# Two-layer streaming step: the heads' stage as four lanes, and written order on all engines between the layers

## The chip, the cores and the metric

The kernel runs on 1 core of one Trainium2 chip. The metric is the device time of one execution in microseconds, as the median of several runs. Engines are called as in the profile: PE (TensorE, matmuls), DVE (VectorE), ACT (ScalarE), POOL (GpSimd) and SP (SyncE, which here only issues DMAs). POOL issues DMAs too.

## The reference

A step of a two-layer encoder over 640 tokens (a prompt of 512 and 8 running streams of 16), with D = 2048, in fp32. Layer 0 is stick-breaking attention with 16 heads. Layer 1 is gated linear attention (GLA) with 4 heads, keys of 256 and values of 512 per head. What the change touches is the end of layer 0 and layer 1:

```
h = rmsnorm(x, norm_g[i]) * (1 + scale) + shift
q, k, v, r, a_lr = split(h @ w_in)                       # layer 1
g = log_sigmoid(a_lr @ w_a2 + b_a) / 16                  # decay, b = cumsum(g) in a chunk
a = tril((q * exp(b)) @ (k * exp(-b)).T)
o = a @ v + (q * exp(b)) @ S
S = exp(b_last) * S + (k * exp(b_last - b)).T @ v
o = o * rsqrt(mean(o * o)) * g_out
y = (o * silu(r)) @ w_out
x = x + gate * y
```

The outputs are y, the new keys and values of layer 0, the final GLA state of the prompt, and the 8 updated states of the streams (8 x 4 heads x 256 x 512 floats, read and written).

## The kernel before

**Arithmetic.** An fp32 product is three matmuls of halves: high x high, high x low, low x high. `halves(hi, lo, x)` (L133) makes them: ACT casts x to hi (L134), DVE subtracts hi from x (L135). Weights come as raw pieces of 128 x 1024 (`wr`, two slots) and are split into `wh`, `wl` by the same pair.

**Stages.** (1) The input is loaded, turned and scaled, and the modulation vectors are computed (to about 165 us). (2) `by_sevens` multiplies by the input weights of layer 0 with seven products in place of eight: it works on sums and differences of quarters of h and of the weights (L514), to about 960 us. `Quarters` holds the parts of h, and `add_up` makes the sums (`sx`, L410) and their halves (`sums`). (3) Attention runs between the first three shares of layer 0's output projection (to about 1450 us). A `share` (L588 on, products L602) is one quarter of the inner dimension of the output projection: four column blocks, in each of them five token tiles, two weight pieces. (4) The last share of layer 0 adds gate and residual (`add`, three DVE operations, L1126 to L1128), squares on ACT (`junk`, L1131), and `turn` brings the tiles into columns (L1112, L1114). `norm` makes the reciprocal root mean square of a tile: a reduce and a mean square on DVE, a power on POOL (L229, `nrm_r`), a widening on DVE (L236), a turn on PE (L238). `scaled` (L244 to L250) applies norm, scale and shift: DVE and ACT for the prompt's part, POOL for the sample's part. (5) `six` (L448) makes the values of GLA head 0 in eight pieces j, `low` (L1189) makes a_lr, `plain` (L560) makes the queries of head 0. (6) `by_sevens` of layer 1 (1660 to 2089 us) makes the other projections by a list of `jobs`: keys, queries, then for each head gates and values. Values are turned into rows by PE (`as_rows`, L583) and stored. (7) The heads' stage (2089 to 2587 us): the rest of the queries and keys by `plain` as filler, then shares 0 to 2 of the layer's output projection as filler, and between their matmuls the four GLA heads. (8) The last share with the final norm (L1652, to the end).

**The order of the work.** PE follows the written order in the whole kernel. A planner (`Side`) counts an estimated PE clock `pe["now"]` while the program is written: lanes (generators) yield `step(wait, tp, z, tiled)`, that is, when they may go on and how many banks of accumulators they need, and `drive` places them between the matmuls of the filler. `side.until` lets the lanes run without a filler. DVE, ACT, POOL and SP take an order that a scheduler derives from the written program; this order is fixed in the built program. `load` and `store` issue DMAs on SP (L70, L73), `move` issues them on POOL (L77).

**The heads before.** A generator `heads` takes the heads one after the other: `decayed` (decays of one head), then `prompt_lane` (four blocks of 128 tokens: L1323, L1311) and `sample_lane` side by side. `sample_lane` handles 16 groups of states in all: four `s0` tiles of 128 x 512 are read (six buffers, loads on SP), multiplied with the queries (L1522) and updated (L1528, DVE L1530), then stored by POOL. `normed` normalizes an output (`on`, with a power on POOL, `on_r`), and `leave` turns it (L1344) and multiplies it with the gates `sr` (L1346). When a head is done, its four rows of blocks (`og`) go to memory or, for the last head and half of heads 1 and 2, straight into halves (`ogh`, `ogl`). `fetch_og` reads the stored ones back before a share.

## Time and profile before

| what | value |
|---|---|
| median of 3 runs | 2663.24 us (2654.84 to 2666.6) |
| the profiled execution | 2674.77 us |
| its span | 2673.1 us |
| its mean granted clock of PE | 0.966 |
| PE busy | 2491.7 us (93%) |
| DVE busy | 1607.2 us (60%) |
| ACT busy | 1005.3 us (38%) |
| POOL busy | 218.0 us (8%) |
| DMA | 498.58 MB, mean 187 GB/s |

The profile is of one execution, which took 11.5 us more than the median. A row of the timeline gives start, length, engine, line, operation, output and inputs, count, and in brackets the idle time of the engine before it with what ended it. A row of waits gives the sum of such idle times, how often, and the longest. Line numbers are those of the kernel before.

### The profile page before, as it was taken

The numbers are of one execution on the slowest core, as the hardware profiler recorded it, in microseconds if no ns is written. First come the engines' busy times: TensorE is split into PE (matmuls) and PEld (weight loads), VectorE is DVE, ScalarE is ACT, GpSimd is POOL, SyncE is SP. The second block draws the span as 40 slices with busy tenths as digits, with TensorE's granted clock in tenths as the row PEclk, the third lists the DMA queues.
The fourth block names the chain that finished last, engine by engine and source line by source line (L and its number), as shares of the span: only waits on it lengthen the run. The fifth ranks groups of instructions, "written<-read, shape, count | busy, mean of one in ns | idle before, by whom it ended". The sixth has DMA issues, their size and how long they took to land.

```text
span 2673.1 us, 43709 instructions
## 1 busy us (share of the span) xinstructions
PE 2491.7 (93%) x17393; PEld 2167.2 (81%) x17393; DVE 1607.2 (60%) x2398; ACT 1005.3 (38%) x1756; POOL 218.0 (8%) x440
## 2 busy tenths in 40 slices
PE   6889999999999989999999789999999799799877
PEld 4569999989999988777777658999999778576655
DVE  4555555565556646666775683666667454455557
ACT  4332222222223335565443452333333334352333
POOL 1200000000000000000000340000000121212113
PEclk8899999999999999999999989999999899899998
DMA  9966666766664376667665533333443666657354
GB/s 324 308 211 212 224 202 214 231 201 217 218 211 139 105 236 214 215 216 244 198 208 165 168 92 107 104 113 106 130 135 104 212 210 216 196 171 225 124 172 162
DMA packets 495549, 498.58 MB, mean 187 GB/s; under 512 B 25130, under 2 KB 415666, under 8 KB 494706
## 3 DMA queue, kind: packets, MB, share of 16 engines
q1 hardware_dynamic: 486066, 465.90, 55.5%
q0 software_dynamic: 9280, 29.89, 3.2%
q8 instruction: 137, 2.24, 0.3%
q14 instruction: 66, 0.54, 0.1%
HBM read 408.54 MB, written 87.16 MB: 185 GB/s over the span
## 4 chain that ended last, share of the span: by engine, by line
PE 74%; DVE 7%; DMA 7%; issue 5%; POOL 3%; ACT 2%; SPq 1%; POOLq 0%; ACTq 0%; DVEq 0%
PE ps_mm L514 41%; PE ps_mm L602 11%; PE ps_mm L560 3%; PE ps_mm L448 3%; PE ps_tp L956 2%; DMA s<-in_state_gla_dram 1%; SPq L70 1%; PE ps_z L900 1%; PE ps_tp L924 1%; PE ps_z L177 1%; PE ps_z L217 1%; DMA ar<-in_w_ada_dram 1%; PE ps_z L969 1%; PE ps_tp L1001 1%; PE ps_tp L1311 1%
## 5 line engine op out<-in xcount | busy, mean ns | idle before, releaser
L514 PE MATMUL ps_mm<-sums,wh 128*128 128x320 f32 x2880 | 643.4, 311 | 2.7 <-ACT wh L134 2.7
L514 PEld LDWEIGHTS ps_mm<-sums,wh 128*128 128x128 f32 x2880 | 480.6, 188 | 14.8 <-issue 9.5
L514 PE MATMUL ps_mm<-h,wh 128*128 128x320 f32 x2160 | 482.7, 311 | 0.6 <-ACT wh L134 0.3
L514 PE MATMUL ps_mm<-sums,wl 128*128 128x320 f32 x1440 | 445.8, 310 | 1.4 <-DVE wl L135 1.4
L135 DVE TENSOR_TENSOR wl<-wr,wh 128x1024 fp32r<-128x1024 f32 x195 | 239.6, 1230 | 251.1 <-ACT wh L134 247.3
L514 PEld LDWEIGHTS ps_mm<-h,wh 128*128 128x128 f32 x2160 | 359.2, 188 | 16.1 <-issue 10.4
L134 ACT CAST wh<-wb 128x1024 fp32r<-128x1024 f32 x180 | 188.9, 1049 | 466.5 <-PE ps_mm L514 401.3
L134 ACT CAST wh<-wr 128x1024 fp32r<-128x1024 f32 x195 | 204.3, 1049 | 385.6 <-PE ps_mm L514 202.4
L514 PE MATMUL ps_mm<-h,wl 128*128 128x320 f32 x1080 | 333.8, 309 | 0.7 <-DVE wl L135 0.7
L514 PEld LDWEIGHTS ps_mm<-sums,wl 128*128 128x128 f32 x1440 | 271.0, 188 | 1.9 <-DVE wl L135 1.9
L135 DVE TENSOR_TENSOR wl<-wb,wh 128x1024 fp32r<-128x1024 f32 x180 | 220.0, 1222 | 63.3 <-ACT wh L134 62.8
L602 PE MATMUL ps_mm<-wh,ogh 128*128 128x512 f32 x530 | 233.4, 440 | 26.4 <-ACT ogh L134 19.0
L560 PE MATMUL ps_mm<-h,wh 128*128 128x320 f32 x896 | 209.8, 322 | 11.4 <-DVE kr L135 8.8
L602 PE MATMUL ps_mm<-wh,ogl 128*128 128x512 f32 x530 | 212.7, 401 | 1.5 <-DVE ogl L135 1.2
L602 PE MATMUL ps_mm<-wl,ogh 128*128 128x512 f32 x530 | 212.3, 401 | 0.0
L514 PEld LDWEIGHTS ps_mm<-h,wl 128*128 128x128 f32 x1080 | 202.8, 188 | 1.0 <-DVE wl L135 1.0
L560 PEld LDWEIGHTS ps_mm<-h,wh 128*128 128x128 f32 x896 | 153.8, 194 | 19.7 <-issue 16.4
L602 PEld LDWEIGHTS ps_mm<-wh,ogh 128*128 128x128 f32 x530 | 102.9, 194 | 61.7 <-ACT ogh L134 22.4
L560 PE MATMUL ps_mm<-h,wl 128*128 128x320 f32 x448 | 141.5, 316 | 0.0
L448 PE MATMUL ps_mm<-wh,h 128*128 128x512 f32 (+1 forms) x320 | 114.5, 429 | 19.2 <-DVE h L135 10.9
L602 PEld LDWEIGHTS ps_mm<-wh,ogl 128*128 128x128 f32 x530 | 102.2, 193 | 27.6 <-DVE ogl L135 4.6
L602 PEld LDWEIGHTS ps_mm<-wl,ogh 128*128 128x128 f32 x530 | 103.4, 195 | 13.3
(297 smaller groups left out, 3730.8 us busy)
## 6 DMA issues: line engine op xcount, KB each, us to landing
ar<-in_w_ada_dram SPq DMA_DIRECT2D x160, 512.0 KB
wb<-in_sb_w_in_dram SPq DMA_DIRECT2D x84, 512.0 KB
kc<-in_cache_sb_k_dram SPq DMA_DIRECT2D x64, 512.0 KB
vc<-in_cache_sb_v_dram SPq DMA_DIRECT2D x64, 512.0 KB
wb<-in_gla_w_in_dram SPq DMA_DIRECT2D x51, 512.0 KB
wr<-in_gla_w_in_dram SPq DMA_DIRECT2D x45, 512.0 KB
wr<-in_sb_w_in_dram SPq DMA_DIRECT2D x44, 512.0 KB
ar<-in_w_ada_dram SPq DMA_DIRECT2D x64, 256.0 KB
```

What stands on the lines that cost most here:

```text
L70: nc.sync.dma_start(out=out, in_=in_)
L134: nc.scalar.copy(hi, x)
L135: dve.tensor_tensor(lo, x, hi.bitcast(F32), op=ALU.subtract)
L177: mm(acc[32 * q:32 * q + 32, :w], cT[:, kt + m, :], by(cT[:, kt + m, :], rs[m // each][:, m % each, q, :]), start=kt + m == 0, stop=kt + m ...
L217: mm(acc[32 * j:32 * j + 32, :256], cT[:, kt + m, :], by(cT[:, kt + m, :], r[:, 256 * j:256 * j + 256]), start=kt + m == 0, stop=kt + m == ...
L448: mm(acc[i][:n, :], l, by(l, r[:, e, :]), start=j == 0 and e == 0 and first, stop=j == 7 and e == 1 and last)
L514: mm(acc, l[:, k, :], by(l[:, k, :], r), start=start and k == 0 and first, stop=k == 7 and last, skip_group_check=True)
L560: mm(acc[nt], l[:, k, :], by(l[:, k, :], r), start=i == 0 and k == 0 and first, stop=i == 1 and k == 7 and last)
L602: mm(acc, l, by(l, r[:, e, :]), start=i == 0 and e == 0 and first, stop=i == 1 and e == 1 and last)
L900: mm(z[:, :n], q[:, hh, qs], by(q[:, hh, qs], k[:, hh, :n]), start=True, stop=True)
L924: mm(o[:, :P], l, by(l, aT[:, kb, :]), start=kb == 0, stop=kb == qb)
L956: turn_block(tp[:, P * c:P * c + P], block(kc[:, c, P * hh:P * hh + P]), ident)
```

## The change

1. *Written order on all engines but SP.* From the last share of layer 0 to the last `add_up` of layer 1's h, DVE, ACT and POOL now follow the written order too (`in_order`). The code there is rearranged: `norm` issues its power before it yields for the bank, `scale` runs one j ahead of `part_up`, the first `add_up` stands before the queries, the other seven between their matmuls (before: from inside `six` on), and the load of the decays' weights stands ahead of `six`.
2. *`plain`* takes a list of parts and fetches and splits the next weight piece in the middle of the present one.
3. *The jobs* of layer 1 make the values of heads 1 to 3 first and the gates last.
4. *The heads' stage* has four lanes over all heads: `decays` (one head ahead of the others, two buffers for q and k), `prompt_lane`, `sample_lane` and `fetches`. Values and gates are read for each block. Each block's gated output goes to memory at once, for all heads, and `fetches` reads the rows back, one ahead. State tiles have five buffers (before six), and their loads are issued by POOL (`move`) instead of SP.

```diff
-S0 = 6
+S0 = 5
+GP = 1
...
         def norm(a):
+            yield step(3.0)
             ss = po.tile([P, 1], F32, tag="ss", name="ss", bufs=2)
             dve.tensor_reduce(out=ss, in_=ss4[:, a, :], axis=mybir.AxisListType.X, op=ALU.add)
-            yield step(4.0, tp=1)
-            rstd_row(po, ss, bc, a)
+            r = rstd_of(po, ss, D, "nrm")
+            yield step(1.2, tp=1)
+            rstd_wide(po, r, bc, a)
...
+        in_order = ExitStack()
+        in_order.enter_context(tc.manual_schedule(engines={mybir.EngineType.DVE, mybir.EngineType.Activation,
+                                                           mybir.EngineType.Pool}))
         ring3.update(pool=sp, tags=("s0", "s1"))
         fetch_x(0)
         drive(share(3, og0, w_out0, add, lambda c: c < 3 and fetch_x(c + 1), first))
...
+        def make(j):
+            if j < 7:
+                h2.scale(1, j + 1, xT, bc)
+            if j < 8:
+                h2.part_up(1, j)
...
+        h2.scale(1, 0, xT, bc)
+        make(0)
+        acc = [bank("mm") for _ in range(5)] + [bank("z")]
+        def until(j):
+            make(j + 1)
+            if j == 6:
+                halves(wa[:, :, :16], wa[:, :, 16:], r)
...
+        add_up()
+        queries = plain(h2, src, [(P * hh, leave_q(hh)) for hh in range(2)])
...
-        for h in range(GH):
-            jobs += [(2 * NK + D + 512 * h + 256 * n, keep_gate(h, n)) for n in range(2)]
-            if h:
-                jobs += [(2 * NK + 512 * h + 256 * n, keep_value(h, n)) for n in range(2)]
+        jobs += [(2 * NK + 512 * h + 256 * n, keep_value(h, n)) for h in range(1, GH) for n in range(2)]
+        jobs += [(2 * NK + D + 512 * h + 256 * n, keep_gate(h, n)) for h in range(GH) for n in range(2)]
...
-        for hh in range(2):
-            for _ in plain(h2, src, P * hh, leave_q(hh)):
-                if n % 5 == 2:
-                    add_up()
-                n += 1
+        for _ in queries:
+            if n % 4 == 1:
+                add_up()
+            n += 1
         for _ in range(8):
             add_up()
+        in_order.close()
...
-                load(s0, A["state_gla"][0, 2 * m + e, h, P * dt:P * dt + P, :])
+                move(s0, A["state_gla"][0, 2 * m + e, h, P * dt:P * dt + P, :])
...
-                    yield step(max(since, max(states[x][1] for x in group) + 4.5) - pe["now"], tiled=True)
+                    yield step(max(since, max(states[x][1] for x in group) + 7.0) - pe["now"], tiled=True)
...
+            dve.tensor_tensor(g, tp.rearrange("p (s t) -> p s t", s=4), g, op=ALU.mult)
+            move(og_d[h][:, :, t0:t0 + P], g)
...
+        def decays():
+            for h in range(GH):
+                while min(through.values()) < h - 1 or h >= 2 and not came["plain"]:
+                    yield step(0.5)
...
+        def fetches():
...
+            for kt in range(KT):
+                while min(through.values()) <= kt // 4 or not came["last"]:
+                    yield step(0.5)
+                if kt not in rows:
+                    yield step(2.0)
+                    ask_rows(kt)
+                    if kt % 4 < 3 and came["plain"]:
+                        ask_rows(kt + 1)
+                    yield step(4.0)
+                while not free(kt):
+                    yield step(0.3)
+                n = 20 + 2 * kt % 12
+                og1[kt] = slot(n, name="ogh"), slot(n + 1, name="ogl")
+                halves(*og1[kt], rows.pop(kt))
+                if kt % 4 < 3 and kt + 1 not in rows:
+                    ask_rows(kt + 1)
+                came["rows"], came["at"] = kt + 1, pe["now"]
+                yield step(0.5)
...
-        side.add(heads())
+        for x in (decays(), prompt_lane(), sample_lane(), fetches()):
+            side.add(x)
```

How the change moves instructions, at three places. First DVE at the first boundary between column blocks of the last share of layer 0; `ps_mm` is the accumulator of a tile, `y` the partial sum, `xc` the residual, `s1` and `wl` are low halves of weight pieces. Before:

```order
L1126 TENSOR_TENSOR y_11551<-ps_mm_15474,y_11551 128x512
L1127 TENSOR_TENSOR y_11551<-y_11551,gate_bc_15371 128x512
L1126 TENSOR_TENSOR y_11559<-ps_mm_15475,y_11559 128x512
L1128 TENSOR_TENSOR y_11551<-y_11551,xc_15367 128x512
L135 TENSOR_TENSOR wl_15542<-wr_15537,wh_15541 128x1024
L1127 TENSOR_TENSOR y_11559<-y_11559,gate_bc_15371 128x512
L1126 TENSOR_TENSOR y_11700<-ps_mm_15565,y_11700 128x512
L1128 TENSOR_TENSOR y_11559<-y_11559,xc_15369 128x512
```

(The split into `s1` stands one row ahead of these.) In the changed kernel, with its own line numbers:

```order
L1146 TENSOR_TENSOR y_11539<-ps_mm_15464,y_11539 128x512
L1147 TENSOR_TENSOR y_11539<-y_11539,gate_bc_15361 128x512
L1148 TENSOR_TENSOR y_11539<-y_11539,xc_15357 128x512
L1146 TENSOR_TENSOR y_11547<-ps_mm_15465,y_11547 128x512
L1147 TENSOR_TENSOR y_11547<-y_11547,gate_bc_15361 128x512
L1148 TENSOR_TENSOR y_11547<-y_11547,xc_15359 128x512
L136 TENSOR_TENSOR s1_15524<-wr_15381,s0_15523 128x1024
L136 TENSOR_TENSOR wl_15532<-wr_15527,wh_15531 128x1024
L1146 TENSOR_TENSOR y_11688<-ps_mm_15555,y_11688 128x512
```

The split of the next block's second weight piece (`s1`) has moved from ahead of the last two tiles' adds to behind all of them, and the split after it (`wl`) with it.

Second, POOL at the end of that share and the start of `six`; `xp` is a sample part of h, `nrm_r` the power of a norm. Before:

```order
L229 TENSOR_TENSOR nrm_r<-nrm_ms,mhalf 128x1 x2
L246 TENSOR_TENSOR xp<-xp,rstd_bc_15360 128x128 x9
L249 TENSOR_TENSOR xp<-xp,sc_83 128x128
L246 TENSOR_TENSOR xp<-xp,rstd_bc_15360 128x128 x3
L249 TENSOR_TENSOR xp<-xp,sc_83 128x128 x3
L246 TENSOR_TENSOR xp<-xp,rstd_bc_15360 128x128 x2
L249 TENSOR_TENSOR xp<-xp,sc_83 128x128 x5
L229 TENSOR_TENSOR nrm_r<-nrm_ms,mhalf 128x1
```

And in the changed kernel (the last three rows go on in the same way for all 16 parts):

```order
L852 MEMSET k_15110 128x1
L230 TENSOR_TENSOR nrm_r<-nrm_ms,mhalf 128x1 x5
L249 TENSOR_TENSOR xp<-xp,rstd_bc_15348 128x128
L252 TENSOR_TENSOR xp<-xp,sc_83 128x128
L252 TENSOR_TENSOR xp<-xp,sh_82 128x128
```

The five powers have moved ahead of all the scaling, and the scaling goes part by part.

Third, POOL in the heads' stage, within the states of head 0; `s` is a state tile, `out_dram` the output, `on_r` the power of an output's norm. Before:

```order
L77 DMA out_dram<-s_21214 128x512
L77 DMA out_dram<-s_21216 128x512
L77 DMA out_dram<-s_21765 128x512
L77 DMA out_dram<-s_21774 128x512
L229 TENSOR_TENSOR on_r<-on_ms,mhalf 128x1
L77 DMA out_dram<-s_21793 128x512
```

And in the changed kernel:

```order
L78 DMA out_dram<-s_21872 128x512
L78 DMA s_22008<-in_state_gla_dram 128x512
L78 DMA out_dram<-s_21922 128x512
L78 DMA s_22011<-in_state_gla_dram 128x512
L78 DMA s_22046<-in_state_gla_dram 128x512
L230 TENSOR_TENSOR on_r<-on_ms,mhalf 128x1
L78 DMA s_22048<-in_state_gla_dram 128x512
L78 DMA gk_109<-pl 128x640
```

The loads of states, which stood in SP's order before, now stand in POOL's order between the stores and the powers.

More of the change, by code (lines that the diff above doesn't have):

```diff
@@ L1536, in hybrid_step_kernel @@
-        came = {"heads": 0, "free": False}
-        def heads():
-            for h in range(GH):
-                while h == 2 and not came["free"]:
-                    yield step(0.5)
-                d = {}
-                yield from decayed(h, d)
-                both = [prompt_lane(h, d), sample_lane(h, d)]
-                for x in both:
-                    side.add(x)
-                while any(x[0] in both for x in side.lanes):
-                    yield step(0.5)
-                for s in range(4):
-                    if h == GH - 1 or h and s < 2:
-                        og1[4 * h + s] = og_slots(4 * h + s)
-                        halves(*og1[4 * h + s], d["sr"][:, s, :])
-                    else:
-                        move(og_d[4 * h + s], d["sr"][:, s, :])
-                came["heads"] = h + 1
@@ L1577, in hybrid_step_kernel @@
             for g in range(GH - 1):
-                side.until(lambda: came["heads"] > g)
-                for s in range(4):
-                    fetch_og(4 * g + s)
+                side.until(lambda: came["rows"] >= 4 * g + 4 and pe["now"] > came["at"] + 2.0)
                 drive(share(g, og1, w_out1, first=first))
+                came["shares"] = g + 1
                 first = [wraw(w_of(g + 1, 0, i), 2, 512) for i in range(2)]
```

427 lines of the change are left out of this document (232 added, 195 removed).

## The prediction

> **What bounds the kernel now.** I read the page first, then the waits of TensorE (PE) in the two stretches that the change touches, then single rows there.
>
> ```profile
> PE 2491.7 (93%) x17393; PEld 2167.2 (81%) x17393; DVE 1607.2 (60%) x2398; ACT 1005.3 (38%) x1756; POOL 218.0 (8%) x440
> PE   6889999999999989999999789999999799799877
> ```
>
> PE is busy for 93% of a span of 2673.1 us, so it bounds the program, and at most 181 us are idle. Each digit is 66.8 us. The digits below 9 lie in the first 200 us, from 1470 to 1604 us (a 7 and an 8), and in the last 600 us. The change reorders nothing before about 1453 us, so I compare two stretches: A, from the last share of layer 0 to the first products of sums (1453 to 1670 us), and B, the heads' stage (2087 to 2607 us). The matmul work is the same in both kernels (9336 rows of PE before, 9337 after): the time can move only through idle PE, and through the clock that follows idleness.
>
> Stretch A, one window of 10 us and one of 50 (columns: length, PE, PEld, DVE, ACT, POOL busy, clock, DMA share, GB/s) and PE's waits (sum, times, longest):
>
> ```profile
> 1540.00:1550.00 10.00, 1.22 (x2) 0.50 (x2) 10.00 (x14) 10.00 (x21) 2.23 (x2) 0.50 0.83 222
> ...
> 1600.00:1650.00 50.00, 50.00 (x288) 41.59 (x287) 13.21 (x16) 11.38 (x18) 0.00 (x0) 1.00 0.43 119
> ...
> PE ps_mm L448 <- DVE h L135: 8.3, 1, 8.3
> PE ps_tp L238 <- DVE rstd_w L236: 6.9, 2, 5.7
> PE ps_tp L238 <- DVE nrm_ms L227: 6.6, 1, 6.6
> ```
>
> Stretch B, the same list of waits, and three rows of the timeline (start, length, group, idle time before it):
>
> ```profile
> PE ps_mm L602 <- ACT ogh L134: 16.7, 6, 5.2
> PE ps_z L1522 <- DMA s<-in_state_gla_dram: 15.2, 13, 3.2
> PE ps_mm L1652 <- ACT wh L134: 9.3, 2, 4.9
> PE ps_mm L560 <- DVE kr L135: 8.8, 1, 8.8
> PE ps_mm L602 <- DVE y L607: 4.3, 4, 3.2
> PE ps_tp L1378 <- DVE wa L1358: 3.5, 1, 3.5
> ...
> 2494.86 0.79 PE L602 MATMUL ps_mm<-wh,ogh 128*128 128x512 f32 x1 [3.16 <-DVE y L607]
> 2496.30 0.63 PE L602 MATMUL ps_mm<-wh,ogh 128*128 128x512 f32 x1
> 2496.73 0.63 PE L602 MATMUL ps_mm<-wl,ogh 128*128 128x512 f32 x1
> ```
>
> The last three rows show what a gap costs beyond itself. After 3.16 us of idleness matmuls start 0.43 us apart (2496.30 to 2496.73). Undisturbed they start 0.23 us apart (the rows of 1466.75 and 1466.98 us, below). About seven matmuls are slow, so a gap of about 3 us costs some 7 x 0.20 = 1.4 us more. I add this to each long gap.
>
> **The change, part by part, stretch A.** *(1) The norms' chain, a gain of 8.* PE waited 6.6 us for the norm of one tile. GpSimd (POOL) shows why:
>
> ```profile
> 1511.39 4.79 POOL L246 TENSOR_TENSOR xp<-xp,rstd_bc 128x128 f32<-128x128 f32 x9
> 1522.40 0.55 POOL L229 TENSOR_TENSOR nrm_r<-nrm_ms,mhalf 128x1 f32<-128x1 f32 x1
> 1523.55 0.77 PE L238 MATMUL ps_tp<-ident,rstd_w 128*128 128x128 f32 x2 [6.58 <-DVE nrm_ms L227]
> ```
>
> POOL scales the sample's columns from 1511.39 us, and the 0.55 us power that PE needs stands behind 23 of these (1511.39 to 1522.40). Written in order, the five powers come first. That removes 6.6 us and the slow matmuls behind it, 1.4: 8. Three norms keep short waits of about 1 us each, because each reduce and power now sits behind three adds (0.7 us each, below): a loss of 3.
>
> *(2) From the last share to `six`, a gain of 9.* The last products of the share end at about 1528.5 us, and `six` runs for good only here:
>
> ```profile
> 1527.52 0.58 PE L602 MATMUL ps_mm<-wh,ogl 128*128 128x512 f32 x1
> 1550.57 1.22 PE L448 MATMUL ps_mm<-wh,h 128*128 128x512 f32 x2 [8.32 <-DVE h L135]
> ```
>
> That is 22 us. In the written order there remain: three adds 2.1, square 0.8, reduce and mean square 0.3, power 0.55, widening 0.3, PE and copy 1.0, then scaling of the first two pieces (two prompt parts 2 x 0.75 on DVE, while POOL does three operations of 0.4 to 0.6 for each), casts and subtractions 2 x (0.73 + 0.83), and semaphores: about 13. The bounds are 0 (each step as late as now) and 14.
>
> *(3) Inside `six`, a gain of 3.* The weights stall once:
>
> ```profile
> 1595.07 0.50 PE L448 MATMUL ps_mm<-wh,h 128*128 128x512 f32 x1 [1.14 <-ACT wh L134]
> 1596.33 0.80 PE L448 MATMUL ps_mm<-wl,h 128*128 128x512 f32 x1 [0.76 <-DVE wl L135]
> ```
>
>  Scaling one piece ahead and taking the add-ups out of this loop gives ACT and DVE room: 1.9, and about 1 of slow matmuls behind. One `wr` slot less costs nothing while load, cast and subtraction (about 4.4 + 1.05 + 1.23 = 6.7 us) stay under the 8.2 us of matmuls for a piece (36 at 0.23).
>
> *(4) The weight split at the share's boundaries, a loss of 16.* This part speaks against the change. Rows of before at a boundary between column blocks:
>
> ```profile
> 1464.70 0.63 ACT L1131 ACTIVATE junk<-y 128x512 bf16<-128x512 f32 x1 [0.56 <-DVE y L1128]
> 1465.23 0.19 ACT L1131 ACTIVATION_READ_ACCUMULATOR junk<-y 128x1 f32 x1
> 1465.58 1.05 ACT L134 CAST s<-wr 128x1024 fp32r<-128x1024 f32 x1 [0.16 <-PE ps_mm L602]
> ...
> 1466.66 1.22 DVE L135 TENSOR_TENSOR s<-wr,s 128x1024 fp32r<-128x1024 f32 x1 [2.06 <-ACT s L134]
> 1467.80 0.68 DVE L1126 TENSOR_TENSOR y<-ps_mm,y 128x512 f32<-128x512 f32 x1
> ...
> 1466.75 0.40 PE L602 MATMUL ps_mm<-wl,ogh 128*128 128x512 f32 x1
> 1466.98 0.40 PE L602 MATMUL ps_mm<-wh,ogl 128*128 128x512 f32 x1
> ```
>
> The split (cast, subtraction) runs ahead of the last adds of its block, and PE does not stop. In the written order it stands behind all five tiles' adds and squares. Call the end of the block's last matmul E. The fourth tile's adds end at E+0.9, the fifth's at E+3.0 (three of 0.7), its square and readout (0.63 + 0.19) at E+3.8, the cast at E+4.85, the subtraction at E+6.1. PE has six matmuls of the other piece (1.4 us) and then needs the cast: idle 3.45, and 0.65 more for the subtraction. With 1.4 of slow matmuls this is 5.5 at each of three boundaries: 16. The bounds are 0 (if ACT comes to the cast before the squares are due) and 18. I take the upper half, because each step is one engine's fixed order and has a measured duration.
>
> *(5) The add-ups during the queries, a loss of 8.* Before, the seven late add-ups ran among `six`, where ACT and DVE had room, and the products of sums started with one stall of 3. Now they stand behind the stores of the values:
>
> ```profile
> 1618.74 0.59 ACT L134 CAST vhi<-ps_mm 128x512 fp32r<-128x512 f32 x1 [2.43 <-DMA gv<-vhi]
> 1636.89 0.88 DVE L1202 TENSOR_TENSOR alr<-ps_tp,alr 32x320 fp32r<-32x320 f32 x2
> ```
>
> This chain ends about 15 us after `six` (1622.5), and ACT and DVE now pass through it before the second weight piece of the queries: that piece is about 4 us late. The sums, four more casts and four subtractions per j at 0.48 us, end 4 to 5 us behind the first products that read them. With a later wait of 1 the phase loses 11 instead of 3. The bounds are 0 and 15.
>
> A sums to 8 - 3 + 9 + 3 - 16 - 8 = -7: a loss of 7, between a gain of 12 and a loss of 25.
>
> **Stretch B.** *(6) Start of the stage, a gain of 16.* The values' last transposes left PE waiting (kr 8.8 and two short waits of 0.5 and 1.0), with about 1.6 of slow matmuls behind. With the gates last there are no transposes at the end. The wait of 3.5 for wa and its 1.5 of slow matmuls go too, because the decays' small weights are fetched a head ahead. That is 10.3 + 1.6 + 3.5 + 1.5 = 17, less 1 for the plain piece's own first wait. The bounds are 8 and 17.
>
> *(7) The shares' starts, a gain of 13.* Here the rows `og` of the head come back through memory one at a time:
>
> ```profile
> 2270.62 0.32 SPq L70 DMA_DIRECT2D og_in<-og  x1
> 2274.22 0.72 ACT L134 CAST ogh<-og_in 128x640 fp32r<-128x640 f32 x1 [1.36 <-DMA og_in<-og]
> ...
> og<-sr POOLq DMA_DIRECT2D x8, 320.0 KB, 4.1
> ```
>
> 3.6 us pass from issue to cast, and PE waits for each of the first rows (6 waits, 16.7). Afterwards a lane reads the rows one ahead into two buffers, as soon as a head is through, the plain pieces are done and a slot is free. All four rows of a head now go this way (before: two of four for heads 1 and 2, none for the last), which adds eight loads of about 3.6 us on SP, beside other work. Of the 16.7 with 0.8 for ogl and about 5 of slow matmuls (22), I keep 9 for the fetches that start once the plain pieces have ended, where PE has only the lanes. The y waits (4.3) are left as they are. The bounds are 0 and 22.
>
> *(8) The end, a gain of 3.* Two wh waits (9.3) come from four casts of og that stand ahead of the weights' cast. In the changed kernel the last head's rows must land and come back: turning 0.7, multiplication 0.7, store issue 0.55, landing 4.1, read 3.6, split 1.6, about 12 us, against 60 matmuls that remain as cover (13.7 us). The rows of before put half of the waits (4.7) with 1.4 of slow matmuls on the og casts: 6 go, and 3 come back. The bounds are -8 and 12.
>
> *(9) States, a gain of 5.* Loads of states move from SP to POOL:
>
> ```profile
> SPq L70 <- DMA out_dram<-s: 146.1, 54, 10.9
> POOL out_dram L77 <- DVE s L1530: 124.8, 44, 10.9
> ...
> out_dram<-s POOLq DMA_DIRECT2D x64, 256.0 KB, 3.2
> ```
>
> SP stood for 146.1 us in 54 waits until a store had landed. That wait frees SP for weights and rows, and it moves to POOL, which already waits 124.8 us for the states' updates. Each load there costs an issue of 0.55 us (64 x 0.55 = 35 us of POOL, no PE time) and can hold up to 3.2 us of landing ahead of the norms' powers. The order spaces states further ahead (7 us against 4.5), which should shorten the 15.2 us of waits on them. The bounds are -15 (one landing late at each of the five norms of one head) and 15.
>
> B sums to 16 + 13 + 3 + 5 = 37, between about 10 and 55. The parts together: 37 - 7 = 30 us. The profiled execution took 2674.8 us, which would become 2645. It lies 11.5 us above the median of the runs shown (2663.24), so on the median's scale I forecast 2633.
>
> **The rivals.** *POOL's queue is the new bound (slower).* POOL runs in order: stores wait for updates, the loads behind them wait for a landing, and the powers `on_r` behind both. If each of the 20 norms came 3.2 us late at PE (20 x 3.2 = 64, against 4.0 us that PE waits on `on` now), then 2633 + 64 = 2697. It decides from about 2.2 us at each norm (44 us). For it: the 146.1 us above. Against it: POOL is busy for 8% of the span, and head-to-head lanes give other work to PE. Chance 0.12.
>
> *Stretch A gives back most of it (no change).* The boundaries cost 18, the add-ups 15, the tail gains nothing: A loses 25, B gains its lower 20, so 2663 + 5 = 2668, or 2658 with 30 in B. For it: every step of part 4 has its row. Chance 0.15.
>
> *The add-ups' GpSimd part is starved.* Rows of before:
>
> ```profile
> 1561.30 8.72 POOL L410 TENSOR_TENSOR sx<-xp 128x320 f32<-128x320 f32 x2 [3.41 <-DVE sums L135]
> 1570.45 1.07 POOL L410 TENSOR_TENSOR sx<-xp 128x320 f32<-128x320 f32 x1 [0.43 <-DVE sums L135]
> ```
>
> The same operation took 4.4 us where DVE was full, and 1.07 later. If all 16 run at 4.4, POOL needs 70 us for add-ups beside 28 us of queries and at most 20 of covered products: 22 more lost, 2655. [...] Against it: DVE is busy for 13.2 of the 50 us from 1600 us on, in which the queries lie. Chance 0.08.
>
> *Both stretches gain (boundaries hidden).* Without part 4, and with the upper bounds of 6 and 7, about 25 us better: 2608. Chance 0.15.
>
> **How the numbers follow.** The forecast has a chance of 0.50, with its own range of 2615 to 2650. This kernel can tell about 0.5% from no change, 13 us: faster means below 2650, slower above 2676.5. Faster: nearly all of the forecast (0.47), the last rival (0.15), and a share of the next-to-last (0.03): 0.65. Slower: POOL's queue (0.12) and a little of A giving back (0.02): 0.14. The rest, 0.21, is no change. The range for 8 in 10 goes from 2602 to 2675.
>
> **What would show it.** In the changed profile: PE waits of 3 to 4 us on the weights' cast at three places of the last share of layer 0 (part 4). No wait on the mean square, and `six` some 9 us closer to the share's end. No wait on kr at the start of the heads' stage, and ogh waits of at most 10 us. POOL's queue waiting on landed stores, and PE's wait on `on` not above 10 us. The prediction is wrong if the last of these grows to tens of microseconds, or if the windows of the heads' stage keep 68 idle microseconds.

## The result and the profile after

The changed kernel took 2675.33 us (median of 20 runs, 2668.34 to 2681.04), the kernel before 2667.43 us beside it (20 runs, 2654.84 to 2677.65). The ratio is 1.0025, with a 95% interval of 1.0014 to 1.0037: a little slower, and less than the 0.5% that the prediction called telling. The forecast was 2633 us, with 2602 to 2675. Three executions in the experiments below took 4051 to 9650 us, far longer than the others of their kernels, and the ratios leave them out.

```profile
PE 2491.7 (93%) x17393; PEld 2164.2 (81%) x17393; DVE 1617.4 (61%) x2426; ACT 1018.9 (38%) x1804; POOL 268.3 (10%) x516
PE   6989999999999989999999889999999998788986
```

PE is busy for the same 2491.7 us, and the low digits are still there. The profiled execution of the changed kernel has a span of 2670.3 us, less than the 2673.1 of before, although the medians stand the other way round. One execution differs from the next by several microseconds: the heads' stage of before (first plain to end of share 2) took 475.7 us in the profile shown, and 468.8, 467.3 and 470.9 in three later runs with the old heads' stage (the second of them with five state buffers instead of six). So I read single profiles by stage and take verdicts from medians only.

The stages, from the first and last starts of the groups of matmuls (us). The four kernels are before, changed, and the two halves of the change that the first two experiments ran alone:

| | before | changed | new heads only | written order only |
|---|---|---|---|---|
| end of `low` | 1631.6 | 1631.5 | 1634.9 | 1630.5 |
| from there to the first products of sums | 34.2 | 40.5 | 34.3 | 40.1 |
| first products of sums to the end of `by_sevens` | 423.4 | 426.2 | 425.8 | 424.3 |
| end of `by_sevens` to the first plain | 12.1 | 0.9 | 1.0 | 11.2 |
| first plain to the end of share 2 | 475.7 | 483.3 | 485.0 | 468.8 |
| end of share 2 to the final share | 10.2 | 1.8 | 1.5 | 10.3 |
| the final share | 67.5 | 68.0 | 67.0 | 65.6 |

The first stretch ends where it did, and 6 us are lost behind it. The heads' stage begins and ends 20 us tighter. In between it is 8 us longer than in the profile of before, and 13 to 14 us longer than the 471 us that the old stage took on average (the four numbers above). PE's idle time in 489 us around the stage is 56.1 us, against 58.5 before: most of it is still there.

PE's waits between the layers in the changed kernel (sum, times, longest):

```profile
PE ps_mm L452 <- ACT wh L135: 5.9, 1, 5.9
PE ps_mm L617 <- ACT wh L135: 5.6, 2, 2.8
PE ps_mm L573 <- DVE wl L136: 3.9, 3, 1.7
PE ps_mm L518 <- ACT wh L135: 3.8, 1, 3.8
PE ps_tp L241 <- DVE rstd_w L239: 3.2, 4, 1.0
PE ps_tp L241 <- DVE ss L1138: 3.1, 1, 3.1
PE ps_mm L617 <- ACT s L135: 2.8, 1, 2.8
```

The first boundary of its last share, in the timelines of ACT, of DVE and of PE:

```profile
1471.99 0.63 ACT L1151 ACTIVATE junk<-y 128x512 bf16<-128x512 f32 x1 [0.80 <-DVE y L1148]
1472.53 0.19 ACT L1151 ACTIVATION_READ_ACCUMULATOR junk<-y 128x1 f32 x1
1472.62 1.03 ACT L135 CAST s<-wr 128x1024 fp32r<-128x1024 f32 x1
```

```profile
1471.21 0.69 DVE L1148 TENSOR_TENSOR y<-y,xc 128x512 f32<-128x512 f32 x1
1473.68 1.23 DVE L136 TENSOR_TENSOR s<-wr,s 128x1024 fp32r<-128x1024 f32 x1 [1.78 <-ACT s L135]
```

```profile
1470.48 0.40 PE L617 MATMUL ps_mm<-wh,ogl 128*128 128x512 f32 x1
1473.70 0.50 PE L617 MATMUL ps_mm<-s,ogh 128*128 128x512 f32 x1 [2.82 <-ACT s L135]
1474.96 0.79 PE L617 MATMUL ps_mm<-s,ogh 128*128 128x512 f32 x1 [0.76 <-DVE s L136]
```

The long waits on the norms' powers and on h are gone; short ones remain (3.2 us in four, and 3.1 on the sum of squares). In their place stands the weights' cast: the last add ends at 1471.9, the square and its readout at 1472.7, the cast follows, and PE stands from 1470.9 to 1473.7. The same pair of waits stands at all three boundaries (2.82 and 0.76, 2.83 and 0.76, 2.82 and 0.57).

PE's waits in the heads' stage of the changed kernel:

```profile
PE ps_z L1597 <- DMA s<-in_state_gla_dram: 25.8, 18, 4.0
PE ps_mm L617 <- ACT ogh L135: 12.4, 2, 11.6
PE ps_tp L1573 <- DVE kd L1566: 5.7, 2, 5.1
PE ps_mm L1726 <- ACT wh L135: 5.4, 1, 5.4
PE ps_tp L1417 <- DVE wa L1404: 4.4, 1, 4.4
```

The start of the stage, and the one long wait for rows, from the timelines of PE, SP and ACT:

```profile
2099.14 0.54 PE L573 MATMUL ps_mm<-h,wh 128*128 128x320 f32 x2 [0.68 <-DVE out L524]
...
2301.38 0.32 SPq L71 DMA_DIRECT2D og_in<-og  x1
2312.77 0.72 ACT L135 CAST ogh<-og_in 128x640 fp32r<-128x640 f32 x1 [6.96 <-DMA og_in<-og]
```

What SP's and POOL's DMA queues waited for there:

```profile
SPq L71 <- DMA og<-gate: 132.9, 18, 20.3
POOL s L78 <- DMA out_dram<-s: 44.8, 25, 4.3
```

The wait at the start is 0.7 us. The waits for rows are two instead of six, but one of them is 11.6 us: the row asked for at 2301.4 is there only at 2312.8, 11.4 us later, where 3.6 us were read off before. The waits for states have grown from 15.2 to 25.8 us, and the wait for `kd` is new. SP's queue now stands behind gate tiles whose store has not landed (132.9 us), POOL's behind stores of states (44.8 us).

### The profile page after: what moved, and what is told of

It is laid out like the page before. It is cut to its first block, busy times and chain, and to the rows that moved or that the text cites. A ratio compares the mean times of both kernels' runs of the same rounds, so it can differ in the third digit from the quotient of the medians.

```text
span 2670.3 us, 43803 instructions
## 1 busy us (share of the span) xinstructions
PE 2491.7 (93%) x17393; PEld 2164.2 (81%) x17393; DVE 1617.4 (61%) x2426; ACT 1018.9 (38%) x1804; POOL 268.3 (10%) x516
## 4 chain that ended last, share of the span: by engine, by line
PE 72%; DMA 11%; DVE 7%; issue 5%; POOL 2%; ACT 2%; SPq 1%; POOLq 0%; ACTq 0%; DVEq 0%
PE ps_mm L518 40%; PE ps_mm L617 11%; PE ps_mm L452 4%; PE ps_mm L573 3%; PE ps_tp L972 2%; DMA s<-in_state_gla_dram 1%; DMA ar<-in_w_ada_dram 1%; PE ps_tp L940 1%; SPq L71 1%; PE ps_z L916 1%; PE ps_z L218 1%; DVE wl L136 1%; PE ps_z L178 1%; PE ps_tp L1017 1%; PE ps_z L985 1%
## 5 line engine op out<-in xcount | busy, mean ns | idle before, releaser
L573 PEld LDWEIGHTS ps_mm<-h,wh 128*128 128x128 f32 x896 | 153.7, 194 | 14.8 <-issue 10.6
```

What stands on the lines that cost most here:

```text
L573: mm(acc[nt], l[:, k, :], by(l[:, k, :], r), start=k0 == 8 and k == 0 and first, stop=k0 == 0 and k == 7 and last)
```

## The experiments

All times are medians of 5 to 12 runs; the ratio is to the kernel before on the same chip. Two changes of about 4 us lie at the edge of what such a comparison tells.

**The two halves apart.** First the new heads' stage, jobs and prefetch with the old stretch between the layers (the diff is against the changed kernel).

```diff
-        in_order = ExitStack()
-        in_order.enter_context(tc.manual_schedule(engines={mybir.EngineType.DVE, mybir.EngineType.Activation,
-                                                           mybir.EngineType.Pool}))
...
-            r = rstd_of(po, ss, D, "nrm")
-            yield step(1.2, tp=1)
-            rstd_wide(po, r, bc, a)
+            yield step(4.0, tp=1)
+            rstd_row(po, ss, bc, a)
...
-        for _ in queries:
-            if n % 4 == 1:
-                add_up()
-            n += 1
+        for hh in range(2):
+            for _ in plain(h2, src, [(P * hh, leave_q(hh))]):
+                if n % 5 == 2:
+                    add_up()
+                n += 1
```

> The changed kernel with the stretch between the layers put back as it was before (scheduler's order, old norm, add-ups from inside six on); the heads' stage, the list of jobs and the prefetch of plain stay changed. Theory 1 (the written order costs time between low and the first sums, the heads' stage gains a little): about 8 us faster than before, because the two profiles show the start of the stage 11 us and the end 8 us shorter, the stage itself 8 us and the seven-product stage 3 us longer. Theory 2 (the four lanes are what costs, and the profiled execution of the changed kernel hid it): slower than before by about 8 us, as the whole change is.

2666.85 us, ratio 1.0009 (0.9994 to 1.0023). Neither theory's number: the four lanes make no difference that can be measured. The table shows a gain of 20 at the two ends of the stage, and 14 us more between them than the 471 us that the old stage took on average. Then the opposite: the changed stretch between the layers, with the old jobs and heads' stage.

```diff
-        jobs += [(2 * NK + 512 * h + 256 * n, keep_value(h, n)) for h in range(1, GH) for n in range(2)]
-        jobs += [(2 * NK + D + 512 * h + 256 * n, keep_gate(h, n)) for h in range(GH) for n in range(2)]
+        for h in range(GH):
+            jobs += [(2 * NK + D + 512 * h + 256 * n, keep_gate(h, n)) for n in range(2)]
+            if h:
+                jobs += [(2 * NK + 512 * h + 256 * n, keep_value(h, n)) for n in range(2)]
...
-        for x in (decays(), prompt_lane(), sample_lane(), fetches()):
-            side.add(x)
+        side.add(heads())
```

> The kernel before with only the stretch between the layers changed (written order on DVE, ACT and POOL, new norm, add-ups in the queries, prefetch in plain within one part); heads' stage and jobs as before. Theory 1: slower than before by 6 to 8 us, all of it between the end of low and the first products of sums (first sums at about +6 us, end of low at +0). Theory 2: no change, within 2 us.

2672.1 us, ratio 1.0033 (1.0021 to 1.0045): 7 to 9 us slower, as theory 1 had it. The loss of the changed kernel comes from the changed stretch between the layers, taken as a whole. The new norm, the places of the add-ups and the prefetch changed with the written order in it, and this run does not part them.

**Gates last, alone.**

```diff
-        for h in range(GH):
-            jobs += [(2 * NK + D + 512 * h + 256 * n, keep_gate(h, n)) for n in range(2)]
-            if h:
-                jobs += [(2 * NK + 512 * h + 256 * n, keep_value(h, n)) for n in range(2)]
+        jobs += [(2 * NK + 512 * h + 256 * n, keep_value(h, n)) for h in range(1, GH) for n in range(2)]
+        jobs += [(2 * NK + D + 512 * h + 256 * n, keep_gate(h, n)) for h in range(GH) for n in range(2)]
```

> The kernel before with only the list of jobs changed (values of heads 1 to 3 first, gates last). If the transposes of the last values are what PE waited for at the start of the heads' stage, the wait of 8.8 us with its slow matmuls goes: 8 to 11 us faster than before. The rival: the values' stores or the gates' work on DVE and ACT make the seven-product stage longer by the 3 us seen in the changed profile, and the wait for the decays' weight comes earlier and grows: 0 to 4 us faster.

2665.65 us, ratio 1.0002 (0.9990 to 1.0013). The rival was right, and the waits of this kernel's heads' stage say how:

```profile
PE ps_mm L602 <- ACT ogh L134: 16.2, 5, 5.6
PE ps_z L1520 <- DMA s<-in_state_gla_dram: 11.8, 8, 2.5
PE ps_tp L1376 <- DVE wa L1356: 11.7, 1, 11.7
```

The wait on kr (8.8) is gone. The wait on wa has grown from 3.5 to 11.7: PE begins the plain matmuls 8 us earlier (2093.4 instead of 2101.3) and waits at the first decay for the same small weights. SP issues their loads only when the stage has begun, hardly earlier than before. From SP's timelines of the kernel before and of this one:

```profile
2106.94 4.34 SPq L70 DMA_DIRECT2D wa2r<-in_gla_w_a_dram  x6
...
2104.03 6.04 SPq L70 DMA_DIRECT2D wa2r<-in_gla_w_a_dram  x6
```

The first decay starts at 2115.1 us, at 2116.3 in the kernel before. This is the first head, and no head runs ahead of it in which its weights could be fetched.

**The weights split ahead of the last adds.** In the changed kernel, the second piece of the next column block is split as soon as its slot is free. The written order stays.

```diff
-            ws = [w0, made()]
+            ws = [w0, w1 if early and c else made()]
...
                 for i in range(2):
+                    if i and early and c < 3:
+                        w1 = made()
                     for a in (3, 4):
                         yield from products(acc[a], a, i, ws[i])
```

> The changed kernel, where the second weight piece of the next column block in the last share of layer 0 is split ahead of the fourth and fifth tiles' adds (as soon as its slot is free) instead of behind them. Theory (part 4 of the prediction): the three waits of 2.8 and 0.6 to 0.8 us go with their slow matmuls, 10 to 14 us faster than the changed kernel, so about 2663. Rival: the adds now come later behind the split and the time returns as waits of the norms or of six: within 3 us of the changed kernel.

2656.61 us, ratio 0.9973 (0.9962 to 0.9983). Against the changed kernel's 1.0025 this is 0.52%, 14 us. `low` ends at 1614.9 instead of 1631.5 us. PE's waits between the layers no longer hold the boundaries' casts. Four of those that are left:

```profile
PE ps_mm L452 <- ACT wh L135: 5.5, 1, 5.5
PE ps_mm L518 <- ACT wh L135: 3.7, 1, 3.7
PE ps_mm L573 <- DVE wl L136: 3.5, 3, 1.7
PE ps_mm L617 <- DVE s L136: 0.6, 1, 0.6
```

Of the second, 2.3 us stood in the kernel before as well; the other 1.4 and the third line (3.5) go with the add-ups, as a later run shows. The next runs build on this early-split kernel.

**States loaded by SP again.**

```diff
-                move(s0, A["state_gla"][0, 2 * m + e, h, P * dt:P * dt + P, :])
+                load(s0, A["state_gla"][0, 2 * m + e, h, P * dt:P * dt + P, :])
```

> The early-split kernel (the one that took 2656.6 us) with the loads of states issued by SP again (the tile's buffers stay five, the planner's 7 us stay). Theory 1 (POOL's queue holds the loads behind stores that have not landed: 44.8 us of such waits in the changed profile): PE's wait for states falls from 24 us towards the 12 to 15 us of the old heads' stage, 8 to 10 us faster than the early-split kernel, about 2648. Theory 2 (the rate is set by the buffers and by landings, whoever issues): within 3 us. Theory 3 (SP, which already stands 130 us behind gate tiles that wait for their own store, would hold the states longer): slower by more than 5 us.

2651.9 us, ratio 0.9953 (0.9938 to 0.9967): about 5 us faster than the early-split kernel, between the two theories' numbers, and the two intervals nearly touch. PE's waits on states fall from 23.6 to 20.0 us only, so the order in POOL's queue is a small part of them.

**Two buffers for gates, four for states.**

```diff
-S0 = 5
-GP = 1
+S0 = 4
+GP = 2
```

> The early-split kernel with two buffers for gate tiles and four for states (the same memory). If SP's queue behind the gate tile (132.9 us in 18 waits on its store) delays values and rows that PE needs, ogh's wait of 6 to 12 us shrinks and the kernel gets 3 to 8 us faster. If state buffers are the scarce thing, PE's wait for states grows by 10 us or more and the kernel gets slower by that.

2680.06 us, ratio 1.0058 (1.0037 to 1.0080): 23 us slower than the early-split kernel.

```profile
PE ps_z L1599 <- DMA s<-in_state_gla_dram: 37.4, 26, 3.8
```

The waits on states grow by 14 us. All 64 states pass in 357 us (2139.0 to 2496.4), against 325 in the early-split kernel (2138.2 to 2463.6): 10% more, where a lane that went by the number of its buffers alone would take 25% more. The run changes two things at once, so neither the price of four buffers nor the worth of a second gate buffer can be read from it by itself.

**The written order ended with the last share.**

```diff
         side.finish()
+        in_order.close()
         only_d.close()
...
-            make(j + 1)
-            if j == 6:
-                halves(wa[:, :, :16], wa[:, :, 16:], r)
+            make(j + 2)
+            if j >= 6:
+                add_up()
```

> The early-split kernel, where the written order on DVE, ACT and POOL ends with the last share and its norms; six, low, the add-ups and the queries stand as in the kernel before, in the scheduler's order. Theory (part 5 of the prediction): the written add-ups behind the values' stores cost 4 to 6 us in the queries and at the first sums, so 4 to 6 us faster than the early-split kernel, about 2651, queries 28 us long instead of 32. Rival: without the written order the norms' and scaling's work mixes again at the start of six, and 6 to 10 us come back there: slower by up to 5 us.

2676.93 us, ratio 1.0040 (1.0022 to 1.0057): 18 us slower than the early-split kernel, worse than the rival's number. (`low`, the queries and the other add-ups stand as before too.) Its queries take 28 us again. But the scheduler, free again behind the share, puts the scaling of the sample's parts between the norms' powers. POOL's timeline, and PE's wait:

```profile
1521.30 4.69 POOL L249 TENSOR_TENSOR xp<-xp,rstd_bc 128x128 f32<-128x128 f32 x9 [2.45 <-ACT rstd_bc L242]
1530.54 0.54 POOL L230 TENSOR_TENSOR nrm_r<-nrm_ms,mhalf 128x1 f32<-128x1 f32 x1
```

```profile
PE ps_tp L241 <- DVE rstd_w L239: 16.5, 3, 14.5
```

This is the stall of part 1, larger (14.5 us). It supports part 1's cause, and shows that the written order must reach over the norms and the scaling at the start of `six`; how far beyond them it is needed is not shown.

**Later due times in the lanes** (first head's decays, kd, states).

```diff
-                yield step(4.0)
+                yield step(4.0 if h else 12.0)
...
-                yield step(3.0, tp=1)
+                yield step(8.0, tp=1)
...
-                    yield step(max(since, max(states[x][1] for x in group) + 7.0) - pe["now"], tiled=True)
+                    yield step(max(since, max(states[x][1] for x in group) + 10.0) - pe["now"], tiled=True)
```

> The early-split kernel, where the planner counts on the data later, by about what PE was seen to wait: the first decays' weights 8 us later, kd's turn 5 us later, states 10 us after their request instead of 7. If the lanes only stand too early in PE's order, PE's waits on wa (5 us), kd (5 us) and part of those on states (24 us) are filled with shares' matmuls: 10 to 15 us faster than the early-split kernel. Rival: the lanes are a chain of their own, so that moving them later lengthens the lanes and the last head ends after the filler: no gain, or a few us slower, with a longer wait at the end of the stage.

2648.35 us, ratio 0.9939 (0.9920 to 0.9959): 8 to 9 us faster than the early-split kernel. The way was not as expected. The waits on wa (5.3) and on ogh (6.2) are gone and kd's is 4.2 in place of 5.1, but the waits on states are 28.1 us, more than the 23.6 without these edits.

**Five buffers in the old stage.**

```diff
-S0 = 6
+S0 = 5
```

> The kernel before with five buffers for states instead of six, nothing else. Theory (the state buffers are the scarce thing of the heads' stage; going from five to four took 23 us in the changed stage): PE's wait for states grows from 12 to 15 us to 22 to 28 us, and the kernel gets 8 to 12 us slower. Rival (the old stage had slack, the longer waits on states come from the lanes): within 3 us of before.

2664.66 us, ratio 0.9998 (0.9987 to 1.0010), and PE's waits on states are 10.9 us. The theory falls: one buffer fewer costs the old stage nothing that can be measured.

**Gates last, with the first decays later, in the old stage.**

```diff
             y = gl.tile([P, 2, T], F32, tag="y", name="y")
-            yield step(5.0)
+            yield step(5.0 if h else 17.0)
```

> The kernel before with gates last in the list of jobs, as in the run of that change alone (no change in time, PE's wait on wa grown from 3.5 to 11.7 us), and with the first head's decays due 12 us later in the planner. If the transposes' wait had only moved to wa, that wait falls under 2 us and the kernel gets 8 to 11 us faster than before, about 2655. Rival: the first head starts later, and the same time is missing where share 0 waits for its rows (16 us of waits on ogh grow): within 3 us of before.

2681.1 us, ratio 1.0057 (1.0039 to 1.0074): 15 us slower, beyond the rival. The list of PE's waits:

```profile
PE ps_mm L602 <- ACT ogh L134: 32.0, 8, 11.6
PE ps_mm L560 <- ACT pl L1268: 9.9, 1, 9.9
```

The wait on wa is gone, and at the same place stands the second line, 9.9 us for the copy of a plain piece (1.7 in the run with the jobs alone). The first decay does not start later than there (2113.2 us, 2115.1 there). The waits on ogh have doubled, from 16.2 to 32.0, and the first head's first row is stored 10 us later (2230.8, 2220.4 there), although share 0 itself starts 5 us earlier. Which of these costs the 15 us is not separated.

**The first add-ups inside `six`.**

```diff
         def until(j):
             make(j + 1)
             if j == 6:
                 halves(wa[:, :, :16], wa[:, :, 16:], r)
+            if j >= 4:
+                add_up()
...
-        add_up()
         queries = plain(h2, src, [(P * hh, leave_q(hh)) for hh in range(2)])
...
-            if n % 4 == 1:
+            if n % 6 == 1:
                 add_up()
```

> The early-split kernel, still in written order, with the first four add-ups written inside six (one at each of its last four pieces) and the other four between the queries' matmuls. Theory (DVE is full while the queries run, 23.9 of 25 us, and has room in six, 11.6 of 25 us): the waits on wl of 3.5 us in the queries and of 3.7 and 0.7 us at the first sums go, 5 to 7 us faster than the early-split kernel, about 2650. Rival: six itself stalls by as much.

2653.2 us, ratio 0.9950 (0.9932 to 0.9968), 3 to 6 us faster than the early-split kernel, at the edge of what can be told. From the end of `low` to the first products of sums it takes 34.4 us (40.0 without this, 34.2 in the kernel before), and `six` itself is not longer (69.4 us, 69.6 without this). All waits of PE from `six` on to 1690 us:

```profile
PE ps_mm L452 <- ACT wh L135: 5.5, 1, 5.5
PE ps_mm L518 <- ACT wh L135: 2.3, 1, 2.3
PE ps_mm L452 <- DVE wl L136: 0.8, 1, 0.8
PE ps_mm L518 <- DVE wl L136: 0.7, 1, 0.7
```

**Together.** Early split, states by SP, later due times and add-ups inside `six`, in one kernel (the diffs above).

> Early split, states' loads on SP, later due times and add-ups inside six together. If the gains add (15 of the split, 5 of SP, 8 of the due times, 5 of the add-ups against the changed kernel), about 2639. If the due times and the SP loads remove the same waits on states, about 2643 to 2648.

2640.48 us, ratio 0.9907 (0.9890 to 0.9925): the gains add, within the noise (2639 was expected). This kernel is 0.9% faster than the one before and 1.2% faster than the changed one. Its heads' stage takes 471 us between its ends, the length of the old one, and it keeps the tight ends (1.0 and 4.2 us). What still stands in that stage:

```profile
PE ps_z L1600 <- DMA s<-in_state_gla_dram: 21.7, 12, 3.6
PE ps_tp L1606 <- DMA kst<-k: 6.8, 2, 5.9
PE ps_tp L1606 <- issue: 5.4, 1, 5.4
```

**States due later still.**

```diff
-                    yield step(max(since, max(states[x][1] for x in group) + 10.0) - pe["now"], tiled=True)
+                    yield step(max(since, max(states[x][1] for x in group) + 18.0) - pe["now"], tiled=True)
```

> The kernel with everything together (2640.5 us), with states due 18 us after their request instead of 10. In the changed kernels all states pass between about 2154 and 2488 us, in the kernel before between 2151 and 2559. If PE waits for states because the sample lane runs faster than states can be stored and loaded, a later due time fills these waits (21.7 us) with shares' matmuls: 8 to 15 us faster, about 2630. If the loads take as long as the lanes give them, waits stay near 20 us and the time within 3 us.

2639.29 us, ratio 0.9894 (0.9877 to 0.9910): no change. The waits on states stay (20.8 us), and the states' products span 319 us in both runs (2142.8 to 2462.0, and 2141.2 to 2460.4). The due time does not set the pace of this lane.

**The best stretch with the old stage.**

```diff
-        jobs += [(2 * NK + 512 * h + 256 * n, keep_value(h, n)) for h in range(1, GH) for n in range(2)]
-        jobs += [(2 * NK + D + 512 * h + 256 * n, keep_gate(h, n)) for h in range(GH) for n in range(2)]
+        for h in range(GH):
+            jobs += [(2 * NK + D + 512 * h + 256 * n, keep_gate(h, n)) for n in range(2)]
...
-        for x in (decays(), prompt_lane(), sample_lane(), fetches()):
-            side.add(x)
+        side.add(heads())
```

> The stretch between the layers as in the best form so far (written order, early split, first four add-ups inside six), with the list of jobs and the heads' stage of the kernel before. Theory (the four lanes as written gain nothing against the old stage): as fast as the run with the same stretch and the four lanes, 2653 within 4 us. Rival (the two halves of the change depend on each other): 8 us or more away from it.

2655.45 us, ratio 0.9947 (0.9933 to 0.9962), against 2653.2 with the four lanes: the same. The lanes as written gain nothing beside a good stretch either; with due times and queue mended they gain 11 to 15.

**Only the first decays later.**

```diff
-                yield step(4.0)
+                yield step(4.0 if h else 12.0)
```

> The early-split kernel (2656.6 us), where only the first head's decays are due 8 us later. In the run with three later due times the gain was 8 us. If the wait on wa (5 us with its slow matmuls) is most of it: 5 to 7 us faster than the early-split kernel. If the stage is a chain that starts with the first decays, as it was in the old heads' stage (16 us slower): 5 us or more slower.

2674.36 us, ratio 1.0031 (1.0020 to 1.0042): 15 us slower than the early-split kernel. The waits:

```profile
PE ps_z L1599 <- DMA s<-in_state_gla_dram: 29.6, 15, 7.5
PE ps_mm L1728 <- ACT wh L135: 11.4, 1, 11.4
PE ps_tp L1575 <- DVE kd L1568: 8.9, 1, 8.9
PE ps_tp L1419 <- DVE wa L1406: 0.4, 1, 0.4
```

The wait on wa is gone, kd's is longer, and PE stands 11.4 us before the final share: the last head ends after its cover, as ACT's casts of its rows come only then. The theory of a chain from the first decays to share 0 does not fit, though: share 0 starts 196 us after the first plain matmul (201 in the early-split kernel), and the waits on ogh fall from 6.2 to 3.2. The states' lane is the part that is longer (343 us, against 325). The same edit, together with later due times for kd and the states, gave a gain of 8 to 9. So these edits do not add one by one.

## Why the prediction was wrong

**Stretch A was right.** It was to lose 7 us, and the written order alone loses 7 to 9 (medians, 1.0033).
- Part 4 (16): shown. The boundaries' three pairs of waits sum to 10.6 us, and taking them away gave 14 us with their slow matmuls and what follows. Of its steps, the idle was 2.82 where 3.45 was worked out, and 0.76 where 0.65 was.
- Parts 1 to 3 (8 and -3, 9, 3): PE's stall behind the scaling is gone. From the start of the share's last product until `six` runs for good, 14.2 us pass (1540.2 to 1554.4), where 23.0 passed before (1527.5 to 1550.6): a gain of 8.8, with 9 forecast. That `six` and `low` end where they did fits the sum. That ending the written order early brings the stall back in larger form supports part 1's cause.
- Part 5 (8): 6.3 us by the table, and moving four add-ups gave back 5.6 of them. The three waits on DVE's second weight piece (3.9 us) go with them, so the cause is mainly DVE's time in the queries, as forecast.
- The rival of a starved POOL did not come as a whole. By groups, POOL's 16 operations took 1.35 us each on the mean, less than the 1.76 of before; one of them took 5.28. The rival's reading of its two rows was too quick. Its pair of 8.72 us is one operation of 7.88 and one of 0.88, and how full DVE is does not part slow from fast: DVE was busy for 8.74 of the 10 us from 1560 on, and for 9.97 and 10.00 of the next two tens, in which POOL's operation took 1.06 to 1.12. The slow ones (7.88, 5.35, 5.28) lie beside subtractions of DVE that kept their usual time, and they end as DVE comes to a gap; beside the fast ones DVE's own subtractions of 128 x 320 took up to 1.17 where 0.48 is usual.

```profile
L415 POOL TENSOR_TENSOR sx<-xp 128x320 f32<-128x320 f32 x16 | 21.2, 1347 | 66.1 <-DVE sums L136 66.1
...
L136 DVE TENSOR_TENSOR sums<-sx,sums 128x320 fp32r<-128x320 f32 x28 | 18.9, 729 | 0.0
```

So DVE's side of this was left out of the sum: its subtraction, put at 0.48 us in the prediction, has about that median in both kernels (0.48, 0.49), and a mean of 0.73 in the changed one.

**Stretch B was wrong.** It was to gain 37 us, and the new stage with its jobs gained nothing (1.0009). The two ends of the stage came out: parts 6 (without wa) and 8 had 14 us there, and the table shows 20 less about 3 that `by_sevens` became longer. The step that failed is the middle of the stage. There parts 7 and 9 and the wait on wa were to take out 23 us (13 + 5 + 5), and it became 13 to 14 us longer instead.
- Part 6 (16): the 11 us at the stage's start are real. "The wait of 3.5 for wa ... go too, because the decays' small weights are fetched a head ahead" did not come: the only wait on wa is the first head's, which has no head ahead of it. It is 4.4 us in the changed kernel and 11.7 with the jobs alone. The lengthening of `by_sevens` (423.4 to 425.8 and 426.2) had no term.
- Part 7 (13): 4 to 10. Six waits (16.7 us) became two, 12.4 in the changed kernel and 7.1 and 6.2 in two others with the same stage. In the changed kernel one of the two is as long as three of the old ones, because a row took 11.4 us to come back instead of 3.6.
- Part 8 (3): 8, in the gap before the final share. It was too small.
- Part 9 (5): the sign was wrong, and its reason with it. "The order spaces states further ahead (7 us against 4.5), which should shorten the 15.2 us of waits on them" did not hold: the waits on states are 23.6 to 27.3 us in five profiles of the new stage and 10.9 to 15.2 in five of the old one, and a due time of 18 us instead of 10 changed nothing. The wait on `kd` (5.7 us) had no term at all. The bounds of part 9 (-15 to 15) held its miss, the value taken did not.
- The rival of POOL's queue had its place right and its price wrong. Giving the loads back to SP brought about 5 us, not 64; PE waited for no norm's power.
- About 4 of the 42 us between forecast and result come from the start of the sum: the kernel before had a median of 2663.24 in three runs, and has 2667.43 in twenty. That is the luck of three runs.

**The rule behind these misses.** I added up removed waits of single instructions as if each were on the path by itself. In the heads' stage they were not: PE stands in written order behind whichever lane is late. With the gates last, 8.8 us on kr went and 8 on wa came; with later decays as well, 11.7 on wa went and 8 on a plain piece's copy came. In the whole change, states and `kd` took the place of kr and the rows.

**What stays open.** Why PE waits about 20 us for states in the new stage. The queue explains 4 us, a later due time changes nothing, and five buffers in the old stage cost nothing. The new lane passes its 64 states in 326 us (2154.0 to 2479.7) where the old one took 407, so its buffers come round faster. At the longest of these waits in the changed kernel, the buffers' cycle can be seen, in the timelines of POOL and of PE:

```profile
2247.01 0.54 POOL L78 DMA_DIRECT2D s<-in_state_gla_dram  x1 [1.56 <-DMA out_dram<-s]
...
2249.66 1.92 PE L1597 MATMUL ps_z<-s,qz 128*32 128x512 f32 x2 [4.00 <-DMA s<-in_state_gla_dram]
```

POOL asked for a state only when the store of the buffer's old one had landed, and PE went on 2.65 us later. This is one wait of 18. Against a limit of the buffers alone stands that four of them made the lane only 10% longer, in a run that changed the gates' buffers too. No run separated the buffers' cycle from the traffic of gates and rows beside it, and no run had six buffers in the new stage. Why a row took 11.4 us, and why the wait on `kd` came, was not tested either.

## What to carry to other kernels

A written order fixes the place of everything in it: look at the work behind a long chain of another engine (here a weight split behind five tiles' adds), and write it as early as its slot allows, before judging the order itself. When a wait at the start of a stage is removed, look at the next thing on the same path and ask whether its data come earlier too; if not, the wait only moves. For lanes among filler, changing one due time moves what comes behind it: judge such an edit by the length of the whole stage, not by the wait that it was aimed at, and test several together.

## What the runs showed of the hardware

A subtraction of 128 x 320 on DVE took 0.49 us in the median of the changed kernel, and up to 1.17 us while POOL ran a two-input operation of the same size in 1.07. Where DVE's operations kept their usual time (0.48 us, and 1.22 for 128 x 1024), a single such operation of POOL took 5.28 us in the changed kernel and 7.88 in the kernel before. So here one engine or the other paid, and no run shows what decides which.

A read of 320 KB took 11.4 us from issue to use while the DMA engines moved up to 422 GB/s (in the slice of 1 us at 2307 us; 303 on the mean from 2300 to 2313 us), against 3.6 us for the row of the kernel before that the prediction shows.

PE's matmuls were slow behind some short gaps. In the kernel before, two gaps of 1.14 and 0.76 us with one matmul between them were followed by matmuls 0.43 us apart (0.23 ahead of the changed kernel's boundary), at a granted clock of 0.54 and 0.60 (1596 to 1598 and 1598 to 1600 us). At the first boundary of the changed kernel, gaps of 2.82 and 0.76 us were followed by the same at 0.50 (1475 to 1479 us). Other short gaps of the kernel before did not do this: behind single gaps of 1.04 and 1.40 us (2410.98 and 2558.49 us) matmuls were 0.23 to 0.24 us apart from the fourth on. How many are slow varies too. Behind the 3.16 us gap that the prediction reads, twelve times in a row 0.43 us pass from one matmul to the next, behind one of 3.97 us (2483.75 us) six times, and behind the pairs of gaps at the three boundaries of the changed kernel twelve, seven and twelve times. So the prediction's seven slow matmuls, 1.4 us a gap, fit some gaps and are too few for others.
